# Two transformer blocks on one core: small TensorE products laid out as runs on parts of the array

## The chip, the cores and the metric

One Trainium2 chip, one core of it. A core has TensorE for matrix products (PE in the profile, its weight loads PEld), VectorE (DVE), ScalarE (ACT), GpSimd (POOL) and SyncE (SP), which here issues nearly all the loads. The metric is the device time of one execution in microseconds (us). A time is the median of three executions; beside it stands one profiled execution, with its own time and a span from its first to its last instruction.

## The reference, cut to what matters

Everything is float32; 256 tokens of width 1024 (the "latent" stream x) and 256 tokens of context. First come two layers of a first block, then two layers of a second block:

```
for i in 0, 1:                                   # first block
    x = x + concat(diff_attention, moba_attention) @ w_out[i]
    x = x + conv_ffn(rms_norm(x))                # 1024 -> 2 x 2816 -> 1024
ada[i] = silu(c or c_ctx) @ w_ada[i] + b_ada[i]  # second block: 1024 -> 6144, for latent and context
for i in 0, 1:                                   # shift, scale and gate come from ada[i]
    mix of modulate(x): layer 0 a recurrence (rwkv) and a window attention,
                        layer 1 two attentions that also see the context
    x = x + gate * rms_norm(mix @ w_out_2[i])
    x = x + gate * rms_norm(relu(modulate(x) @ w_ff1[i])**2 @ w_ff2[i])
```

Layer 0 of the second block also runs on the context (its attention, its recurrence, its MLP). q and k of all heads are 64 wide; an attention is q times k transposed, a softmax, and the product with v. A layer of the first block has a "diff" attention (4 heads, each with two score maps, whose difference weighs a v of 128) and a "moba" attention (8 heads of 64).

## The kernel before, in words

The program is traced by a tile framework. A planner then orders each engine's instructions: it takes what is ready by priority (the program's order, unless a context raises it) and by modelled durations and free slots, and each engine runs its list in that order. Two contexts steer it: `tc.issue_after(i)` puts what is traced inside, as far as it is on the engine of `i`, behind `i` in that engine's list (it does not wait for `i` to finish, and it does not hold loads or other engines); `tc.high_priority()` raises the priority.

Buffers come from three lanes, each with named kinds of slots and PSUM banks: `lat` for the latent stream, `cx` for the context, `sd` ("side") for the modulation. A "big" slot holds 128 x 1024 floats, a "mid" slot 128 x 512. Weight matrices are split in two parts (`whi`, `wlo`), and activations too, so that one float32 product takes three passes of products (`proj`, `feat_block`, `down`, lines L292 to L310 and L746 to L748). All other products are plain float32; in the trace such a product is two passes, that is two MATMUL and two LDWEIGHTS records.

What the change touches:

- **Modulation** (`ada`, products on L778). For each of 12 blocks of 512 columns of `w_ada[i]`, eight products, one for each 128 rows: the 32 columns of `sT` (two of them used) against 128 x 512 of weights. Product k writes the 32 partitions `32*(k%4)` on of one PSUM bank, so k and k+4 add up in the same strip. Then a copy (`asb`, L780), four transposes (`adaT`, L784) and a reduction. Argument `a` is the rows of 128 in one load: 2 in `context1` (blocks 0 to 3 of layer 0, big slots of `cx`), 1 in `rest` (its blocks 4 to 11) and in `side` (layer 1, blocks 0 to 9), both in mid slots of `sd`, and 2 in the last two blocks.
- **Scores.** `pad_q` makes two copies of the transposed q, `qa` with zeros below and `qb` with zeros above, so that one head of a pair meets a full 128-row `kT` that holds both heads. Each head takes two products into one bank (`S`: L528 and L529 in `causal_softmax`, L901 in `attend`, L970 in `attend_self`).
- **Values.** The two heads of a pair write the two halves (64 partitions) of one bank: `om` (L647, L648), `oB` (L954 in `attend`, L1001 in `attend_self`).
- **Recurrence** (`rwkv_group`): eight steps, in each of which products of G and uv (L1372) and of AR and the state (L1377) go into one bank, and a later product updates the state (L1417).

The order of the program: `first_norm`, set-ups, `context1`, `first_layer(0)`, `conv_ffn(0)`, `rest`, `first_layer(1)`, `side`, `conv_ffn(1)`, `second_block`. The planner moves parts of `rest`, `side` and the context's work among the rest.

Of the kernel before, what the change touches and what calls it, by code (L numbers as in the profile page):

```python
# [24 lines left out]
CTX = {"cf": 1, "big": 8, "mid": 12, "small": 24, "raw": 4, "whi": 3, "wlo": 3, "wide": 8, "gC": 1}  # L25
SIDE = {"big": 2, "mid": 6, "small": 4}
# [162 lines left out]
class Net:  # L189
# [217 lines left out]
    def pad_q(self, L):  # L407
        nc = self.nc
        qa = L.big([128, 4, 256], name="qa")
        qb = L.big([128, 4, 256], name="qb")  # L410
        nc.gpsimd.memset(qa[64:128], 0.0)
        nc.gpsimd.memset(qb[0:64], 0.0)
        return qa, qb

    def q_T(self, L, xn, gain, qa, qb):

        nc = self.nc
        for t in range(2):
            ps = L.pB("qT")
            pv = ps.rearrange("p (k f) -> p k f", k=4)  # L420
            for j in range(4):
                nc.tensor.transpose(pv[:, j], xn[t][:, j * 128:(j + 1) * 128], self.ident)
            o = slice(t * 128, (t + 1) * 128)
            ga, gb = (gain, gain) if isinstance(gain, float) else (gain[0:64], gain[64:128])
            nc.scalar.activation(qa[0:64, :, o], pv[0:64], AF.Copy, scale=ga)
            nc.vector.tensor_scalar(qb[64:128, :, o], pv[64:128], gb, None, op0=OP.mult)
# [97 lines left out]
    def causal_softmax(self, q, kT, j, bias):  # L524

        nc, L = self.nc, self.lat
        s = L.pA("S")
        nc.tensor.matmul(s[:, 0:128], q[:, j, 0:128], kT[:, j, 0:128], start=True, stop=True)  # L528
        nc.tensor.matmul(s[:, 128:384], q[:, j, 128:256], kT[:, j, 0:256], start=True, stop=True)  # L529
# [24 lines left out]
    def first_layer(self, i, x, act=None):  # L554
# [15 lines left out]
        def qkv(n, jq):  # L570

            qa, qb = self.pad_q(L)
            self.q_T(L, self.head_norm(L, project(n)), self.qg8[:, 2 * i + jq:2 * i + jq + 1], qa, qb)
# [8 lines left out]
            yield qa, qb, kT, v  # L582
# [3 lines left out]
        def diff_att(qa, qb, kT, v, o):  # L586
            def soft(h):
                bias = load_bias(h)
                p0, s0 = self.causal_softmax(qa, kT, h, bias)
                p1, s1 = self.causal_softmax(qb, kT, h, bias)  # L590
# [39 lines left out]
        def moba_att(qa, qb, kT, v):  # L630
            def soft(p):
                ls = []
                for e, q in ((0, qa), (1, qb)):
                    l, s = self.causal_softmax(q, kT, p, load_bias(4 + 2 * p + e))
# [7 lines left out]
            def weigh(p, ls):  # L642
                pts = [self.causal_PT(l) for l in ls]
                o = L.pA("om")
                for e, pt in enumerate(pts):
                    h, oe = 2 * p + e, o[e * 64:(e + 1) * 64]
                    nc.tensor.matmul(oe[:, 0:256], v[:, 0, h * 64:(h + 1) * 64], pt[:, 0:256], start=True, stop=False)  # L647
                    nc.tensor.matmul(oe[:, 128:256], v[:, 1, h * 64:(h + 1) * 64], pt[:, 256:384], start=False,  # L648
                                     stop=True)
# [101 lines left out]
    def ada(self, L, i, a, blocks=range(12)):  # L751
# [19 lines left out]
        for nb in blocks:  # L771
            ps = L.pA("ada")
            for kb in range(0, 8, a):
                raw = (L.big if a == 2 else L.mid)([128, a, 512], name="adaw")
                nc.sync.dma_start(raw, self.plain_rows(w)(kb, a, nb * 512, 512))
                for k in range(kb, kb + a):
                    j = k % 4
                    nc.tensor.matmul(ps[32 * j:32 * j + 32], self.sT[:, k], raw[:, k - kb], start=k < 4, stop=k >= 4)  # L778
            sb = L.mid([128, 512], name="asb")
            nc.scalar.activation(sb, ps, AF.Copy)  # L780

            ps = L.pA("adaT")
            for c in range(4):
# [269 lines left out]
    def rest(self):  # L1053
        for _ in self.ada(self.sd, 0, 1, range(4, 12)):
            pass
# [766 lines left out]
```

## Time and profile before

| | |
|---|---|
| median of 3 runs | 2090.18 us (2087.27 to 2091.03) |
| the profiled execution | 2091.09 us, its span 2089.2 us |
| busy in the span | PE 92%, PEld 76%, DVE 65%, ACT 49%, POOL 45% |
| mean granted TensorE clock | 0.962 |
| DMA | 351.08 MB, mean 168 GB/s |

Busy time of PE is the union of its MATMUL records; records of neighbouring matmuls overlap, so what a group costs PE is read from one start to the next start. "x16" counts MATMUL records, two for each float32 product.

### The profile page before, as it was taken

The numbers are of one execution on the slowest core, as the hardware profiler recorded it, in microseconds if no ns is written. First come the engines' busy times: TensorE is split into PE (matmuls) and PEld (weight loads), VectorE is DVE, ScalarE is ACT, GpSimd is POOL, SyncE is SP. The second block draws the span as 40 slices with busy tenths as digits, with TensorE's granted clock in tenths as the row PEclk, the third lists the DMA queues.
The fourth block names the chain that finished last, engine by engine and source line by source line (L and its number), as shares of the span: only waits on it lengthen the run. The fifth ranks groups of instructions, "written<-read, shape, count | busy, mean of one in ns | idle before, by whom it ended". The sixth has DMA issues, their size and how long they took to land.

```text
span 2089.2 us, 37719 instructions
## 1 busy us (share of the span) xinstructions
PE 1913.3 (92%) x14178; PEld 1591.1 (76%) x14178; DVE 1362.9 (65%) x2855; ACT 1025.7 (49%) x1990; POOL 934.0 (45%) x621
## 2 busy tenths in 40 slices
PE   6989999989998889999898887898699989998998
PEld 4567868888665558899787777787599978776997
DVE  5475388856787645786679878557764467656444
ACT  4455455545454435465465553344454454655443
POOL 3235544693232444444535355545364555113453
PEclk9999999999899999999999999999899999999999
DMA  9857555445455665665563334426465536234562
GB/s 339 309 173 229 155 185 168 151 141 160 144 171 185 189 193 167 196 219 155 176 214 90 103 107 137 135 82 202 152 217 181 188 100 219 71 112 149 184 199 74
DMA packets 270815, 351.08 MB, mean 168 GB/s; under 512 B 43150, under 2 KB 195469, under 8 KB 270632
## 3 DMA queue, kind: packets, MB, share of 16 engines
q1 hardware_dynamic: 267992, 343.32, 51.7%
q0 software_dynamic: 1968, 4.33, 0.7%
q8 instruction: 112, 1.84, 0.4%
q10 hardware_dynamic: 672, 1.02, 0.1%
q14 instruction: 71, 0.58, 0.1%
HBM read 334.04 MB, written 14.55 MB: 167 GB/s over the span
## 4 chain that ended last, share of the span: by engine, by line
PE 44%; DVE 12%; issue 3%; ACT 3%; DMA 2%; POOL 1%; SPq 0%; DVEq 0%; ACTq 0%; POOLq 0%
PE f L310 4%; PE acc L748 3%; PE f L308 3%; PE acc L746 3%; PE acc L747 3%; PE f L309 3%; POOL wlo L269 1%; PE S L901 1%; DVE T L1335 1%; PE up L308 1%; PE g L308 1%; PE up L310 1%; PE g L309 1%; PE g L310 1%; PE up L309 1%
## 5 line engine op out<-in xcount | busy, mean ns | idle before, releaser
L269 POOL TENSOR_TENSOR wlo<-raw,whi 128x1024 fp32r<-128x1024 f32 (+2 forms) x408 | 787.1, 1945 | 985.9 <-ACT whi L265 824.5
L265 ACT ACTIVATE whi<-raw 128x1024 fp32r<-128x1024 f32 (+2 forms) x600 | 507.8, 882 | 139.5 <-issue 35.0
L269 DVE TENSOR_TENSOR wlo<-raw,whi 128x1024 fp32r<-128x1024 f32 x192 | 310.7, 1620 | 108.8 <-ACT whi L265 95.0
L308 PE MATMUL f<-ah,whi 128*128 128x256 f32 x768 | 221.7, 289 | 14.1 <-ACT whi L265 13.9
L310 PE MATMUL f<-ah,wlo 128*128 128x256 f32 x768 | 223.4, 291 | 4.6 <-POOL wlo L269 4.6
L309 PE MATMUL f<-al,whi 128*128 128x256 f32 x768 | 221.3, 288 | 0.3 <-DVE al L383 0.2
L746 PE MATMUL acc<-whi,hh 128*128 128x512 f32 x432 | 168.8, 393 | 2.1 <-ACT hh L461 2.1
L747 PE MATMUL acc<-wlo,hh 128*128 128x512 f32 x432 | 169.2, 392 | 0.0
L748 PE MATMUL acc<-whi,hl 128*128 128x512 f32 x432 | 165.3, 390 | 0.4 <-DVE hl L462 0.4
L308 PEld LDWEIGHTS f<-ah,whi 128*128 128x128 f32 x768 | 149.5, 195 | 17.9 <-ACT whi L265 14.7
L310 PEld LDWEIGHTS f<-ah,wlo 128*128 128x128 f32 x768 | 149.3, 194 | 9.1 <-POOL wlo L269 5.8
L309 PEld LDWEIGHTS f<-al,whi 128*128 128x128 f32 x768 | 149.5, 195 | 2.9 <-DVE al L383 0.8
L1583 DVE TENSOR_TENSOR r<-r 128x512 f32<-128x512 f32 x48 | 39.6, 824 | 126.5 <-ACT r L1582 125.1
L1582 ACT ACTIVATE r<-f 128x512 f32<-128x512 f32 x48 | 28.7, 597 | 186.3 <-PE f L310 179.6
L293 PE MATMUL prj<-wlo,ah 128*128 128x512 f32 (+1 forms) x272 | 107.8, 397 | 3.2 <-DVE wlo L269 2.1
L292 PE MATMUL prj<-whi,ah 128*128 128x512 f32 (+1 forms) x272 | 108.5, 404 | 0.4 <-DVE bt L499 0.4
L310 PE MATMUL g<-ah,wlo 128*128 128x256 f32 x352 | 102.1, 290 | 6.2 <-POOL wlo L269 6.2
L294 PE MATMUL prj<-whi,al 128*128 128x512 f32 (+1 forms) x272 | 105.4, 396 | 1.4 <-DVE al L383 1.4
L778 PE MATMUL ada<-adaw,kept 128*32 128x512 f32 x384 | 98.3, 643 | 8.0 <-DMA adaw<-in_w_ada_dram 7.7
L308 PE MATMUL g<-ah,whi 128*128 128x256 f32 x352 | 102.7, 292 | 0.4 <-DVE kept L786 0.4
L310 PE MATMUL up<-ah,wlo 128*128 128x256 f32 x352 | 101.4, 288 | 1.2 <-POOL wlo L269 1.2
L308 PE MATMUL up<-ah,whi 128*128 128x256 f32 x352 | 102.3, 291 | 0.0
(473 smaller groups left out, 4873.8 us busy)
## 6 DMA issues: line engine op xcount, KB each, us to landing
raw<-in_w_ff_dram SPq DMA_DIRECT2D x128, 512.0 KB, 4.3
raw<-in_w_up_dram SPq DMA_DIRECT2D x88, 512.0 KB, 4.7
adaw<-in_w_ada_dram SPq DMA_DIRECT2D x144, 256.0 KB, 5.0
raw<-in_w_ff_dram SPq DMA_DIRECT2D x128, 256.0 KB, 4.2
raw<-in_w_in_dram SPq DMA_DIRECT2D x48, 512.0 KB, 4.9
raw<-in_w_down_dram SPq DMA_DIRECT2D x44, 512.0 KB, 4.3
adaw<-in_w_ada_dram SPq DMA_DIRECT2D x24, 512.0 KB, 7.5
raw<-in_w_out_dram SPq DMA_DIRECT2D x24, 512.0 KB, 4.2
```

The lines of the kernel that those rows point to most:

```text
L265: nc.scalar.activation(hi, raw, AF.Copy)
L269: eng.tensor_tensor(lo, raw, hi.bitcast(F32), op=OP.subtract)
L292: nc.tensor.matmul(ps[t][:, :n], ah, wh[:, k], start=st, stop=False)
L293: nc.tensor.matmul(ps[t][:, :n], ah, wl[:, k], start=False, stop=False)
L294: self.last = nc.tensor.matmul(ps[t][:, :n], al, wh[:, k], start=False, stop=en)
L308: nc.tensor.matmul(pv[:, j], wh[:, k % a, c], ah, start=first, stop=False, skip_group_check=skip)
L309: nc.tensor.matmul(pv[:, j], wh[:, k % a, c], al, start=False, stop=False, skip_group_check=skip)
L310: nc.tensor.matmul(pv[:, j], wl[:, k % a, c], ah, start=False, stop=k == 7, skip_group_check=skip)
L746: nc.tensor.matmul(acc[t][n], hh[:, k, c], wh[:, n], start=st, stop=False)
L747: nc.tensor.matmul(acc[t][n], hh[:, k, c], wl[:, n], start=False, stop=False)
L748: self.last = nc.tensor.matmul(acc[t][n], hl[:, k, c], wh[:, n], start=False, stop=en)
L778: nc.tensor.matmul(ps[32 * j:32 * j + 32], self.sT[:, k], raw[:, k - kb], start=k < 4, stop=k >= 4)
```

## The change

`ada` asks for all four loads of a block (two rows of 128 each, big slots, of which the side lane now has five), then traces its eight products as one run in the order of rows 6, 7, 4, 5, 2, 3, 0, 1; the copy, the transposes and the reduction after them are at high priority. A run (`Net.run`) puts each product behind the one before it, at high priority. `side` puts the PE instructions of layer 1's modulation behind the last product of `conv_ffn(0)`. q is kept once (`qT`), and `pair_scores` multiplies its upper and lower 64 partitions with those of kT, into two banks, as one run that alternates between the heads, head 1 first. The value products of a pair are runs too, alternating, head 1 first. The lanes `cx` and `sd` get the slot `asb`; `attend_self` is changed as `attend` is. In the recurrence the G products of a step are put behind the state update of the step before.

```diff
-SIDE = {"big": 2, "mid": 6, "small": 4}
+SIDE = {"mid": 4, "small": 4, "big": 5, "asb": 1}
...
-    def pad_q(self, L):
-        qa = L.big([128, 4, 256], name="qa")
-        qb = L.big([128, 4, 256], name="qb")
-        nc.gpsimd.memset(qa[64:128], 0.0)
-        nc.gpsimd.memset(qb[0:64], 0.0)
...
+    def q_T(self, L, xn, gain):
+        q = L.big([128, 4, 256], name="qT")
...
-            nc.scalar.activation(qa[0:64, :, o], pv[0:64], AF.Copy, scale=ga)
-            nc.vector.tensor_scalar(qb[64:128, :, o], pv[64:128], gb, None, op0=OP.mult)
+            if t == 0:
+                nc.scalar.activation(q[:, :, o], pv, AF.Copy, scale=gain)
+            else:
+                nc.vector.tensor_scalar(q[:, :, o], pv, gain, None, op0=OP.mult)
...
+    def pair_scores(self, ss, parts):
+        rows = [slice(e * 64, (e + 1) * 64) for e in range(2)]
+        self.run([lambda o=o, q=q, k=k, e=e, r=r: self.nc.tensor.matmul(ss[e][:, o], q[r], k[r], start=True, stop=True)
+                  for o, q, k in parts for e, r in ((1, rows[1]), (0, rows[0]))])
+
+    def causal_scores(self, q, kT, j):
+        L = self.lat
+        ss = [L.pA("S") for _ in range(2)]
+        self.pair_scores(ss, [(slice(o, o + n), q[:, j, c:c + 128], kT[:, j, 0:n])
+                              for c, o, n in ((0, 0, 128), (128, 128, 256))])
+        return ss
...
             def weigh(p, ls):
...
+                self.run([lambda e=e, kt=kt: product(e, kt) for kt in range(2) for e in (1, 0)])
...
-            for kb in range(0, 8, a):
-                raw = (L.big if a == 2 else L.mid)([128, a, 512], name="adaw")
-                nc.sync.dma_start(raw, self.plain_rows(w)(kb, a, nb * 512, 512))
-                for k in range(kb, kb + a):
-                    j = k % 4
-                    nc.tensor.matmul(ps[32 * j:32 * j + 32], self.sT[:, k], raw[:, k - kb], start=k < 4, stop=k >= 4)
-            sb = L.mid([128, 512], name="asb")
+            raws = []
+            for kb in range(0, 8, 2):
+                raws.append(L.big([128, 2, 512], name="adaw"))
+                nc.sync.dma_start(raws[-1], self.plain_rows(w)(kb, 2, nb * 512, 512))
+            order = [6, 7, 4, 5, 2, 3, 0, 1]
+            self.run([lambda k=k, m=m: nc.tensor.matmul(ps[32 * (m % 4):32 * (m % 4) + 32], self.sT[:, k],
+                                                        raws[k // 2][:, k % 2], start=m < 4, stop=m >= 4)
+                      for m, k in enumerate(order)])
+            with self.tc.high_priority():
+                sb = L.tile("asb", [128, 512], F32, "asb")
...
+        def scores(j, t):
+            ss = [pS("S") for _ in range(2)]
+            self.pair_scores(ss, [(slice(b * 256, (b + 1) * 256), q[:, j, t * 128:(t + 1) * 128], kTs[b](j))
+                                  for b in range(2)])
+            return ss
...
-            for kt in range(4):
-                for e in range(2):
-                    nc.tensor.matmul(o[e * 64:(e + 1) * 64, t * 128:(t + 1) * 128], vs[kt // 2](j, e, kt % 2),
-                                     pts[e][:, kt], start=kt == 0, stop=kt == 3)
+            self.run([lambda kt=kt, e=e: nc.tensor.matmul(
+                o[e * 64:(e + 1) * 64, t * 128:(t + 1) * 128], vs[kt // 2](j, e, kt % 2), pts[e][:, kt],
+                start=kt == 0, stop=kt == 3) for kt in range(4) for e in (1, 0)])
...
-    def side(self):
-        for _ in itertools.chain(self.ada(self.sd, 1, 1, range(10)), self.setup_odd(self.sd)):
+    def side(self, after):
+        self.behind(self.ada(self.sd, 1, range(10)), after)
+        for _ in self.setup_odd(self.sd):
             pass
+    def run(self, products):
+        last = products[0]()
+        for p in products[1:]:
+            with self.tc.issue_after(last.ins), self.tc.high_priority():
+                last = p()
+        return last
...
...
+            with self.tc.issue_after(update.ins) if i else nullcontext():
...
         net.conv_ffn(0, x)
+        end = net.last
         net.rest()
...
-        net.side()
+        net.side(end)
```

## Rows read from the trace of the kernel before

**Rows 1.** The page, part 1: busy us, share of the span, instructions.
```profile
PE 1913.3 (92%) x14178; PEld 1591.1 (76%) x14178; DVE 1362.9 (65%) x2855; ACT 1025.7 (49%) x1990; POOL 934.0 (45%) x621
```
**Rows 2.** Busy by stretch: length, PE, PEld, DVE, ACT, POOL, clock, DMA, GB/s.
```profile
26.00:320.00 294.00, 277.93 (x1593) 204.06 (x1592) 175.62 (x466) 152.82 (x343) 126.39 (x93) 0.98 0.66 218
...
540.00:800.00 260.00, 235.60 (x1559) 155.20 (x1559) 174.13 (x497) 116.73 (x257) 86.36 (x91) 0.92 0.57 180
...
1080.00:1475.00 395.00, 349.68 (x3536) 307.64 (x3535) 288.90 (x582) 184.36 (x417) 198.27 (x134) 0.94 0.43 129
...
1740.00:1875.00 135.00, 131.19 (x814) 103.77 (x813) 82.87 (x247) 80.07 (x186) 31.61 (x16) 1.00 0.44 138
```
**Rows 3.** Busy time by stretch of the modulation's products alone (L778).
```profile
26.00:320.00 294.00, 44.69 (x192) 0.98 0.66 218
...
540.00:800.00 260.00, 49.75 (x160) 0.92 0.57 180
...
1875.00:2089.20 214.20, 3.85 (x32) 0.96 0.47 151
```
**Rows 4.** Busy time by stretch of the products of L901 alone.
```profile
1080.00:1475.00 395.00, 19.41 (x64) 0.94 0.43 129
...
1740.00:1875.00 135.00, 32.80 (x128) 1.00 0.44 138
```
**Rows 5.** PE's timeline from 127.5 us: start us, us, instruction, records.
```profile
127.79 1.05 PE L778 MATMUL ada<-adaw,kept 128*32 128x512 f32 x2
128.77 0.49 PE L528 MATMUL S<-kT,qa 128*128 128x128 f32 x2
...
130.28 1.06 PE L778 MATMUL ada<-adaw,kept 128*32 128x512 f32 x8
131.27 0.38 PE L292 MATMUL prk<-whi,ah 128*128 128x256 f32 x1
```
**Rows 6.** PE's timeline from 72.9 us.
```profile
73.02 1.92 PE L778 MATMUL ada<-adaw,kept 128*32 128x512 f32 x16 [0.35 <-DVE bt L499]
```
**Rows 7.** PE's timeline from 1818 us.
```profile
1818.16 0.43 PE L954 MATMUL oB<-pt,vb 128*64 128x128 f32 x2
1818.52 0.66 PE L933 MATMUL PT<-kept,L 128*128 128x128 f32 x4
...
1819.45 0.59 PE L901 MATMUL S<-kept,qb 128*128 128x256 f32 x2
1819.88 0.59 PE L901 MATMUL S<-kTc,qb 128*128 128x256 f32 x2
...
1820.84 0.54 PE L954 MATMUL oB<-pt,vb 128*64 128x128 f32 x5
...
1821.85 0.70 PE L901 MATMUL S<-kTb,qa 128*128 128x256 f32 x2
...
1829.49 0.54 PE L954 MATMUL oB<-pt,vb 128*64 128x128 f32 x5
...
1830.52 0.66 PE L933 MATMUL PT<-kept,L 128*128 128x128 f32 x4
```
**Rows 8.** PE's timeline from 812 us: products on quarters of the array.
```profile
813.01 0.46 PE L1377 MATMUL P<-kept,AR 64*64 64x64 f32 x16
```
**Rows 9.** The chain from 750 to 800 us, shares by line.
```profile
by line: PE ada L778 26.7%; PE g L308 9.6%; PE g L309 9.2%; PE g L310 8.0%; PE nT L370 5.2%; PE up L309 5.2%; PE up L308 5.2%; PE up L310 4.5%; PE P L1393 3.4%; PE adaT L784 3.1%; PE P L1406 2.5%; ACT sqj L340 2.5%; PE P L1372 2.4%; DVE rst
```
**Rows 10.** The chain from 1262 to 1300 us, shares by line.
```profile
by line: DVE T L1335 41.8%; DVE Ttmp L1333 34.4%; issue 11.2%; DVE cf L1561 6.3%; DVE xs L1387 2.2%; DVE kept L1381 1.9%; DVE r L1583 1.6%; DVE fl L462 1.6%
```
**Rows 11.** Waits, PE and PEld: in total us, times, longest us.
```profile
PEld ada L778 <- DMA adaw<-in_w_ada_dram: 13.9, 15, 2.9
```
**Rows 12.** Loads of the modulation: count, KB each, median us to landing.
```profile
adaw<-in_w_ada_dram SPq DMA_DIRECT2D x144, 256.0 KB, 5.0
...
adaw<-in_w_ada_dram SPq DMA_DIRECT2D x24, 512.0 KB, 7.5
```
**Rows 13.** Busy time by stretch: the start.
```profile
26.00:105.00 79.00, 75.06 (x367) 46.27 (x365) 44.11 (x109) 32.86 (x59) 24.44 (x17) 1.00 0.93 323
```

More of the change, by code (lines that the diff above doesn't have):

```diff
@@ L2 @@
 import math
-from contextlib import ExitStack
+from contextlib import ExitStack, nullcontext
 import numpy as np
@@ L644, in weigh, with product @@
                 o = L.pA("om")
[L645 to L649, printed above, removed]
+                def product(e, kt):
+                    h, q = 2 * p + e, slice(128 * kt, 256)
+                    return nc.tensor.matmul(o[e * 64:(e + 1) * 64, q], v[:, kt, h * 64:(h + 1) * 64],
+                                            pts[e][:, 256 * kt:256 + 128 * kt], start=kt == 0, stop=kt == 1)
+                self.run([lambda e=e, kt=kt: product(e, kt) for kt in range(2) for e in (1, 0)])
                 self.split_to(his[1][:, p], los[1][:, p], o[:, :256])
@@ L748, in down, with ada @@
                 self.last = nc.tensor.matmul(acc[t][n], hl[:, k, c], wh[:, n], start=False, stop=en)
-    def ada(self, L, i, a, blocks=range(12)):
+    def ada(self, L, i, blocks=range(12)):
         self.mark(f"ada{i}")
@@ L938, in attend @@
         groups = [(j, t) for j in range(4) for t in range(2)]
-        now = []
+        now, ss = [], scores(0, 0)
         for e in range(2):
-            now.append(soft(0, 0, e))
+            now.append(soft(ss[e], 0, 0, e))
             yield
@@ L945, in attend @@
             after, pts = [], []
+            ss = scores(*groups[i + 1]) if i < 7 else None
             for e in range(2):
-                if i < 7:
-                    after.append(soft(*groups[i + 1], e))
+                if ss:
+                    after.append(soft(ss[e], *groups[i + 1], e))
                 pts.append(turn(now[e]))
@@ L998, in out @@
             o = L.pA("oB")
-            for kt in range(2):
-                for e in range(2):
-                    nc.tensor.matmul(o[e * 64:(e + 1) * 64, :256], v[:, kt, e * 64:(e + 1) * 64], pts[e][:, kt],
-                                     start=kt == 0, stop=kt == 1)
+            self.run([lambda kt=kt, e=e: nc.tensor.matmul(
+                o[e * 64:(e + 1) * 64, :256], v[:, kt, e * 64:(e + 1) * 64], pts[e][:, kt], start=kt == 0, stop=kt == 1)
+                for kt in range(2) for e in (1, 0)])
             put(chunk0 + j, o[:, :256])
@@ L1053, in rest, with behind @@
     def rest(self):
-        for _ in self.ada(self.sd, 0, 1, range(4, 12)):
+        for _ in self.ada(self.sd, 0, range(4, 12)):
             pass
-    def side(self):
-        for _ in itertools.chain(self.ada(self.sd, 1, 1, range(10)), self.setup_odd(self.sd)):
-            pass
-    def behind(self, steps):
-        with self.tc.issue_after(self.last.ins):
+    def side(self, after):
+        self.behind(self.ada(self.sd, 1, range(10)), after)
+        for _ in self.setup_odd(self.sd):
+            pass
+    def run(self, products):
[4 more added lines that the diff above has]
+        return last
+    def behind(self, steps, after=None):
+        with self.tc.issue_after((after or self.last).ins):
             for _ in steps:
@@ L1614, in context1 @@
         L = self.cx
-        for _ in self.ada(L, 0, 2, range(4)):
+        for _ in self.ada(L, 0, range(4)):
             pass
@@ L1720, in heads @@
         def heads():
-            qa, qb = self.pad_q(L)
             ps = project(0, 512)
             yield
-            self.q_T(L, rows(ps), 0.125, qa, qb)
+            q = self.q_T(L, rows(ps), 0.125)
             yield
@@ L1757, in second_block @@
         self.lat_out(1, act, x)
-        self.behind(self.ada(self.cx, 1, 2, range(10, 12)))
+        self.behind(self.ada(self.cx, 1, range(10, 12)))
         self.lat_mlp(1, x)
```

82 lines of the change are left out of this document (34 added, 48 removed).

## The prediction

> **What bounds the kernel now.** I read the page first. PE is busy for 92% of the span, the next engine, DVE, for 65% [rows 1]. That is an average, so the second view is the busy time by stretch, in the four stretches where the changed products run [rows 2]. The reader should compare PE with the next engine in each. In 26 to 320 us (first layer's attention, with the context's start) PE is busy for 277.9 of 294 us, in 540 to 800 us (second layer's attention) for 235.6 of 260, in 1740 to 1875 us (the last attention) for 131.2 of 135, and no other engine passes 70% in any of them. In 1080 to 1475 us, the recurrence beside the window attention and the context's MLP, PE has 349.7 of 395 us and DVE 288.9, so two engines are close.
>
> The third view, busy time by stretch of one line, says how much of that is work that the change touches: the modulation's products take 44.7 us of the first stretch, 49.8 of the second, and 3.9 at the end, 98.3 in all [rows 3]; the scores of L901 take 19.4 and 32.8 us [rows 4].
>
> The fourth view is PE's timeline, and it carries the argument. A single product of the modulation (two records) takes 1.05 us; four of them (eight records), which write four different strips of the bank, take 1.06 us [rows 5]; eight in a row (one block) take 1.92 us [rows 6]. Strips run side by side, and the array is paid for once. Where the planner has put one product between other work, it pays for the whole array and uses a quarter.
>
> Last, the chain of waits: from 750 to 800 us the modulation's products are 26.7% of it [rows 9], so there they do set the time. From 1262 to 1300 us the chain is DVE's triangular solve (L1333 and L1335, 76%) [rows 10], so there PE's work does not.
>
> **The change part by part.** *Modulation.* Work is not removed, it is packed. A block costs 1.92 us as a run [rows 6]. The first stretch holds 192 records, 12 blocks at 16: 12 x 1.92 = 23.0 instead of 44.7, saves 21.7 us. 540 to 800 us holds 160, 10 blocks: 19.2 instead of 49.8, saves 30.6. The last two blocks (32 records in 3.85 us) are runs already and save nothing [rows 3]. Sum 52.3 us.
>
> *Scores.* A product of 256 columns costs 0.43 us from start to start [rows 7] and one of 128 columns half of that, 0.22 (estimate, same rate). The padded q makes half of each product zeros. After the change two heads use 64 rows each. No row shows two halves of 64 rows with 128 columns. The bounds are: no overlap, saving nothing, and full overlap, half. The nearest row has products on 64 x 64 quarters, 16 records of 64 columns in 0.46 us [rows 8]; at the rate of 0.43 us for two records of 256 columns they would take 16 x 0.054 = 0.86 one after another. So parts with different rows do overlap, and I take full overlap, less a start for each run. That start is read from single products: 1.05 us against 0.86 us for the further four strips of a block (1.92 less 1.06) [rows 5, 6], of which some 0.07 overlaps what follows (the next start is 0.98 after), so 0.12 us a run. L901 has 64 products in 16 groups in the last attention: 64 x 0.43 / 2 = 13.8, less 16 x 0.12, is 11.9. The window attention has 32 in 8 groups: 5.9. In a layer of the first block 8 groups (four heads, four pairs) have two products of each size, 1.30 us (one group with its start is seen to take 1.51, from 128.77 to 130.28 [rows 5]); after, 0.65 + 0.12: saves 0.53 x 8 = 4.2 a layer. The context's four groups: 4 x (0.86 - 0.12) = 3.0. Sum 29.2 us.
>
> The Trainium skill, TensorEngine Tiling (Array Packing), section Tiling Modes, speaks against this part: a change of the tiling mode drains the array. Each of the 44 score runs stands between full products, so by that rule it pays on the way in and out; the 0.12 us a run taken here would be that drain, and without it the sum would be 5.3 us larger. The skill's page TensorE: Matmul & The Clock Gate, Part 3, gives 3.07 times for four row tiles where four were ideal. By that figure a pair would gain 1.54 times and not 2, and the scores would save some 10 us less; no row here shows the pair.
>
> *Values.* In the last attention a group's eight products come as one (0.36 us to the next start) and seven (1.01 us); where all eight come together they take 1.03 us [rows 7]. Saves 0.34 a group: 16 groups, 5.4 us; in the window attention 8 groups, 2.7. The moba pairs issue one head after the other, 1.30 us by the prices above; alternating 0.65 + 0.12: 0.53 x 4 = 2.1 a layer. The context's values I leave out. Sum 12.3 us.
>
> *Loads and slots.* In the side lane the 144 loads of 256 KB become 72 of 512 KB; landing takes 7.5 us for the size used now by the context, 5.0 for the small one [rows 12]. Five big slots hold one block and a quarter, so three loads of the next block wait until a run has freed its four slots; behind them in SP's queue stand the loads of weights, whose slots hold four blocks ahead. PE's wait is what changes most: a run begins with the rows loaded last, so PE, which takes its list in order, meets at most one wait a block, but with all its later products behind it. Before, PE's weight loads waited 13.9 us for these loads, 2.9 at most [rows 11]. I cost it at nothing more: 22 waits of under 1 us would be 10 us or so, and the same planner places the run. If that cover fails, the rival below has the price.
>
> *At nothing:* the zeroing of q leaves POOL, which is idle 55% of the time [rows 1]; q's copies become one for each half of the tokens instead of two; modulation of layer 1 behind the end of `conv_ffn(0)`, since its products stand after 540 us in any case [rows 3]; the high priority of the copy and transposes; and the G products behind the state update. If the last were wrong it would add one such batch (0.6 to 1.1 us, estimate from the 0.46 of rows 8 upward) to each of 7 steps, some 8 us of a chain that other PE work surrounds.
>
> PE work saved by stretch: 26 to 320 us: 21.7 + 4.2 + 2.1 + 3.0 = 31.0. 540 to 800: 30.6 + 4.2 + 2.1 = 36.9. 1080 to 1475: 5.9 + 2.7 = 8.6. 1740 to 1875: 11.9 + 5.4 = 17.3. In all 93.8 us.
>
> What of it reaches the end? Bounds are nothing and all. In the last attention PE is busy 97% and the next engine 61% [rows 2], and I take 0.85: 14.7. In 26 to 320 PE is at 95%, but the loads use 93% of the DMA engines until 105 us [rows 13], and single products of the modulation also filled gaps that will now stand empty; in 540 to 800 PE is at 91% and DVE at 67%, with softmax chains that come forward next. I take two thirds in both: 20.7 and 24.6. In 1080 to 1475 the solve on DVE is late next; a third, 2.9. Sum 62.9 us. The profiled execution took 2091.1 us, so 2028.2; the median is 0.9 below it, so **2027 us**. Its own range is 2005 to 2050.
>
> **The rivals.**
> - *All of it counts.* For it: PE is at 91% or more in three of the stretches [rows 2], and the modulation stands on the chain [rows 9]. Against: the solve [rows 10]. 2090.2 - 93.8 = 1996 us.
> - *Halves by rows do not overlap.* Then the scores give nothing and pay their starts: converted as above, (4.2 + 3.0) x 0.67 + 4.2 x 0.67 + 5.9 / 3 + 11.9 x 0.85 = 19.7, and 44 x 0.12 x 0.75 = 4 more: 2027 + 24 = 2051. Against it: rows 8. A smaller form, the 1.54 times of the skill, lies inside the forecast's range: 10 x 0.67, some 7 us later.
> - *Another bound comes forward* in the two first-block stretches: loads in the first, softmax chains in the second. A quarter instead of two thirds of 67.9 us costs 28: 2055; with nothing there, and only the last attention's 14.7, 2075.
> - *Slower: PE stands at the head of runs.* Loads come later than planned and everything behind a run in PE's list waits. It decides from 62.9 / 22 = 2.9 us of stall a block. At 5.0 us, a landing time [rows 12], 22 blocks cost 110 and leave 47: 2137. For it: DMA is at 93% early on [rows 13], and some waits reached 2.9 us [rows 11]. Against: the mean of those 15 waits is 0.9 us.
>
> **How the numbers follow.** A measurement of this kernel tells a change of about 0.2% (4 us) from none. Chances: forecast 0.55, all of it 0.16, no overlap 0.08, another bound 0.13 (of which 0.04 so strong that no change is seen), slower 0.08. So faster 0.88, same 0.04, slower 0.08. The range leaves out the slower case, the worst of another bound and the far end of all of it: 1988 to 2070.
>
> **What would show it.** The modulation's records in 24 groups of 16, near 46 us of PE in all; L901's successor at half its busy time, 26 us and some; PE's busy total down by about 90 us, its idle time up by about 30. If PE's total falls and the span does not, the conversion was wrong, and the waits before `PT`, `nT` and the first record of each modulation run say where it went. If the paired scores take as long as now, the overlap was wrong. Long waits of PE for `adaw` would mean the slower rival.

## The result and the profile after

The changed kernel takes 2105.5 us (median of 7 runs, 2098.0 to 2115.1) against 2091.0 beside it (7 runs): 1.0071 times, 95% interval 1.0055 to 1.0087. It is slower by some 15 us, where the prediction had it faster by 63. The profiled execution took 2106.56 us, its span is 2104.7.

The page after, part 1 and two rows of part 2 (the span in 40 slices, in tenths):

```profile
PE 1893.6 (90%) x14178; PEld 1598.9 (76%) x14178; DVE 1384.1 (66%) x2847; ACT 1031.9 (49%) x1982; POOL 899.3 (43%) x605
...
PE   6789978999898699999999999798699999998998
...
PEclk9889989999998757999999999899899999989999
```

PE's busy time fell by 20 us only [rows 1], and the clock row dips to 5 near 750 us. Busy time by stretch, the stretches of [rows 2]:

```profile
26.00:320.00 294.00, 256.85 (x1572) 192.42 (x1572) 170.36 (x458) 147.97 (x334) 119.58 (x85) 0.91 0.66 224
540.00:800.00 260.00, 218.96 (x1507) 155.04 (x1507) 171.44 (x466) 108.31 (x248) 94.93 (x104) 0.80 0.53 167
...
1080.00:1475.00 395.00, 356.48 (x3714) 319.45 (x3713) 295.34 (x613) 193.59 (x439) 209.41 (x142) 0.94 0.47 141
1740.00:1875.00 135.00, 125.27 (x820) 96.29 (x819) 93.16 (x270) 79.78 (x190) 32.31 (x19) 0.95 0.38 123
```

The granted clock (third column from the end) fell from 0.98 to 0.91 and from 0.92 to 0.80 in the first two, and from 1.00 to 0.95 in the last. Busy time at half clock hides what was saved, so I split each trace's span in three. **Work** is the time from each PE record's start to the next one's (at most to its own end) times the clock granted then, that is, at full clock; **clock** is what half clock adds; **idle** is the rest between PE's first record and its last (some 19 us of each span stand before and behind them). (Busy time by clock of a windows row gives nearly the work: 214.02 x 0.80 = 171 for the second attention below.)

| span and its parts, us | span | work | clock | idle |
|---|---|---|---|---|
| before | 2089.2 | 1859.3 | 53.6 | 156.8 |
| after | 2104.7 | 1773.5 | 119.6 | 192.4 |

The work fell by 85.8 us, near the 93.8 that the prediction had, though not by its terms alone (see below). Clock took 66.0 of it back and idle 35.6; 101.6 in all, 16 more than was saved. By phase, each ending with the last product of an output projection or of a network: the first attention grew from 265.7 to 278.0, the first network from 267.6 to 287.5, the second attention from 210.9 to 248.6; the second network shrank from 256.4 to 221.3 (the layer-1 modulation has moved), the recurrence's phase from 479.2 to 468.4, its MLP from 210.9 to 203.4, the last attention from 190.0 to 187.9. So 35 us are lost by 1035 us and 19 won after it.

PE's timeline after, at some places (L785 is what L778 was, L523 the score runs, L652 the value runs):

```profile
63.36 1.92 PE L785 MATMUL ada<-adaw,kept 128*32 128x512 f32 x16
...
75.88 3.64 PE L785 MATMUL ada<-adaw,kept 128*32 128x512 f32 x16 [7.39 <-DMA adaw<-in_w_ada_dram]
...
171.70 0.93 PE L523 MATMUL S<-kT,qT 64*128 64x128 f32 x8
...
175.52 0.48 PE L523 MATMUL S<-kT,qT 64*128 64x128 f32 x2
...
176.59 0.92 PE L523 MATMUL S<-kT,qT 64*128 64x128 f32 x6
...
219.89 0.87 PE L652 MATMUL om<-pt,v 128*64 128x256 f32 x8
...
723.54 3.64 PE L785 MATMUL ada<-adaw,kept 128*32 128x512 f32 x16 [3.95 <-DMA adaw<-in_w_ada_dram]
...
733.27 3.35 PE L785 MATMUL ada<-adaw,kept 128*32 128x512 f32 x16 [4.24 <-DMA adaw<-in_w_ada_dram]
...
754.50 1.55 PE L652 MATMUL om<-pt,v 128*64 128x256 f32 x8
...
786.43 0.80 PE L292 MATMUL wo<-whi,yh 128*128 128x512 f32 x1
...
790.01 0.63 PE L294 MATMUL wo<-whi,yl 128*128 128x512 f32 x1
...
791.08 0.40 PE L294 MATMUL wo<-whi,yl 128*128 128x512 f32 x1
```

A block as a run takes 1.92 us as in [rows 6], and 3.64 where PE waited for its loads and the clock had fallen. A score run in one piece takes 0.93; where something stands between its first product and the rest it takes 0.48 and 0.92. From 746.6 to 790 us, behind a wait of 1.6 us, PE idles for 0.1 us and yet runs at half clock: a value run (`om`) takes 1.55 us there, 0.87 at full clock. The stretch as a row:

```profile
746.60:790.00 43.40, 43.31 (x376) 30.26 (x377) 20.22 (x81) 17.13 (x59) 7.48 (x12) 0.50 0.19 51
```

PE's waits after, and then PE's wait for the modulation's loads before:

```profile
PE nT L370 <- DVE xn L362: 42.2, 12, 8.7
PE ada L785 <- DMA adaw<-in_w_ada_dram: 15.6, 3, 7.4
PE kT L429 <- DVE hn L401: 12.1, 2, 6.7
PE qT L415 <- DVE hn L401: 11.5, 3, 5.8
```

```profile
PE ada L778 <- DMA adaw<-in_w_ada_dram: 7.7, 5, 2.6
```

With the weight loads, which waited 13.9 us before [rows 11] and 0.3 after, the waits for these loads are shorter in sum than they were (15.9 against 21.6 us), but PE's stand in three pieces of up to 7.4 us.

### The profile page after: what moved, and what is told of

Same layout as the page of the kernel before. It is cut to its first block, busy times and chain, and to the rows that moved or that the text cites. A ratio compares the mean times of both kernels' runs of the same rounds, so it can differ in the third digit from the quotient of the medians.

```text
span 2104.7 us, 37530 instructions
## 1 busy us (share of the span) xinstructions
PE 1893.6 (90%) x14178; PEld 1598.9 (76%) x14178; DVE 1384.1 (66%) x2847; ACT 1031.9 (49%) x1982; POOL 899.3 (43%) x605
## 5 line engine op out<-in xcount | busy, mean ns | idle before, releaser
L269 POOL TENSOR_TENSOR wlo<-raw,whi 128x1024 fp32r<-128x1024 f32 (+2 forms) x408 | 768.1, 1894 | 1008.3 <-ACT whi L265 947.7
L265 ACT ACTIVATE whi<-raw 128x1024 fp32r<-128x1024 f32 (+2 forms) x600 | 520.1, 886 | 349.4 <-PE f L309 98.0
L269 DVE TENSOR_TENSOR wlo<-raw,whi 128x1024 fp32r<-128x1024 f32 x192 | 264.2, 1377 | 237.1 <-ACT whi L265 227.8
L308 PE MATMUL f<-ah,whi 128*128 128x256 f32 x768 | 222.5, 291 | 10.6 <-ACT whi L265 10.1
L1603 DVE TENSOR_TENSOR r<-r 128x512 f32<-128x512 f32 x48 | 94.7, 1974 | 28.2 <-ACT r L1602 26.1
L309 PE MATMUL g<-al,whi 128*128 128x256 f32 x352 | 103.5, 294 | 3.1 <-DVE al L378 3.1
L752 PEld LDWEIGHTS acc<-whi,hh 128*128 128x128 f32 x432 | 82.0, 190 | 25.4 <-ACT hh L456 9.6
```

The costliest lines, as they stand in the source:

```text
L265: nc.scalar.activation(hi, raw, AF.Copy)
L269: eng.tensor_tensor(lo, raw, hi.bitcast(F32), op=OP.subtract)
L308: nc.tensor.matmul(pv[:, j], wh[:, k % a, c], ah, start=first, stop=False, skip_group_check=skip)
L309: nc.tensor.matmul(pv[:, j], wh[:, k % a, c], al, start=False, stop=False, skip_group_check=skip)
L752: nc.tensor.matmul(acc[t][n], hh[:, k, c], wh[:, n], start=st, stop=False)
L1603: nc.vector.tensor_tensor(r, r, r, op=OP.mult)
```

## The experiments

Ratios are to the kernel before, run beside each. The edits are shown abridged. The theories: **A**, PE's work got too thin where other chains set the length; **B**, the parts of the array themselves lower the clock; **C**, the new order of PE's list costs the time.

**Layout by itself** (e1). A kernel that leaves the network out and runs each kind of product back to back between full ones:

```diff
+        for f, n in ((single, 32), (strips, 32), (pairs, 64), (padded, 64), (values, 128), (turns, 128)):
+            f(n); warm(24)
+        for _ in range(12): pairs(2); turns(8); values(4)      # the last attention's mix
+        for _ in range(12): padded(4); turns(8); values(4)
```

> This kernel leaves the whole network out: it copies x and runs, on PE alone and without waits, stretches of some 20 us of one kind of float32 product each, with full 128x128x512 products between them. Theory A (PE became sparser, the layout is harmless): every kind holds a granted clock of 1.00 in its stretch; a pair of 64-row halves with 256 columns costs 0.43 us, four strips 0.86 to 0.9 us. Theory B (products on parts of the array do not hold the clock even when nothing waits): the stretches of strips, pairs or values fall to 0.50, those of padded products stay at 1.00.

The granted clock is 1.00 through the whole span. Four strips take 0.86 us (27.6 for 32 rounds), as long as one; a pair of halves 0.435 us, as a padded product alone (0.43). In the mix, from start to start:

```profile
353.25 1.09 PE L72 MATMUL val<-w,x 128*64 128x128 f32 x16
354.28 1.13 PE L62 MATMUL pair<-w,x 64*128 64x256 f32 x8
355.34 1.09 PE L78 MATMUL turn<-ident,w 128*128 128x128 f32 x8
356.37 1.09 PE L72 MATMUL val<-w,x 128*64 128x128 f32 x16
```

Two pairs between other products take 1.06 us where alone they take 0.87, so a run pays 0.19 us for its start, not 0.12. The group takes 3.12 us, with padded scores 3.82. B falls, and so does the rival that halves by rows do not overlap. The Trainium skill, TensorE: Matmul & The Clock Gate, Part 3, measured 3.07 times where four were ideal; these two halves reach 2.0 of 2. The Trainium skill, TensorEngine Tiling (Array Packing), Tiling Modes, has a change of mode drain the array; the 0.19 us agrees with that.

**One part at a time** (e2, e3) and **no saving by packing** (e4): the kernel before with the modulation's part; the changed kernel with the modulation as before; the changed kernel with every modulation product 128 columns wide, which then cannot stand beside another:

```diff
-        self.sT = self.keep([128, 8, 32], F32, name="sT")
+        self.sT = self.keep([128, 8, 128], F32, name="sT")
...
-            matmul(ps[32 * (m % 4):32 * (m % 4) + 32], self.sT[:, k], raws[k // 2][:, k % 2], start=m < 4, stop=m >= 4)
+            matmul(ps, self.sT[:, k], raws[k // 2][:, k % 2], start=m == 0, stop=m == 7)
```

> The kernel before with the modulation's part of the change alone (runs, loads, slots, gate). Theory A: PE's work at full clock falls by about 41 us, half of the added half-clock time of the change (150 us in all) appears here, mostly before 130 us and between 560 and 760 us, and the time is within 12 us of before. Theory B: the same fall of the clock, but inside and right behind the runs also where PE does not wait. Theory C (the new order alone costs, whatever the packing): slower than before by 10 us or more, with PE's idle time up by over 25 us.

> The changed kernel with the modulation put back as before (single products, small loads): scores, values and the recurrence's order as changed. Theory A: here the single products still fill PE, so the half-clock time stays near the 159 us of before, and the time falls by 20 to 30 us. Theory B: half-clock time grows in the attention stretches all the same (over 200 us), and the time is within 10 us of before. Theory C: slower than before.

> The changed kernel, but each of the modulation's products uses all 128 columns of the array (96 of them zeros) and the eight of a block add up in one strip, so that a run takes eight times 0.86 us and not 1.9. That is 24 x 5 = 120 us more PE work in the same order. Theory A: the work stands where PE was waiting at the lower clock, so the time grows by clearly less than 120 us, about 30 to 60, and the half-clock time falls from 309 us to under 230. Theory C: the order costs what it cost, half-clock time stays near 300 us, and the time grows by 90 us or more.

The modulation alone: 2101.2 us, 1.0050 (1.0029 to 1.0071). The pairs, with the change's line in the recurrence, which e3 keeps: 2093.7, 1.0021 (1.0009 to 1.0033). So each part is slower by itself. The time of e2 and its idle time, 35 us more than before, fit A and C alike; e3 is slower, as C had it. The wide products: 2172.3, 1.0388 (1.0368 to 1.0408): 121.6 us more work than in the changed kernel cost 67 us, above A's range and below C's. Of these, 56 us are lost before the second attention begins. In the second attention they cost nothing; the row of the kernel before, that of the wide kernel, and that of the changed one:

```profile
533.30:744.20 210.90, 189.78 (x1220) 127.55 (x1218) 151.09 (x436) 96.77 (x218) 76.29 (x75) 0.92 0.55 174
```

```profile
621.40:868.40 247.00, 230.31 (x1569) 155.51 (x1568) 157.34 (x450) 103.28 (x240) 84.50 (x94) 0.97 0.53 167
```

```profile
565.50:814.10 248.60, 214.02 (x1471) 149.95 (x1469) 160.40 (x438) 102.73 (x239) 93.25 (x103) 0.80 0.54 170
```

Some 52 us more work there (224.5 against 172.0, 51 of it the modulation's) fit into the same 247 us: in the order of the changed kernel PE's work does not set that phase's length, and with more of it the clock stays up (0.97 against 0.80). In that phase this is A. The Trainium skill, TensorE: Matmul & The Clock Gate, section HAM oscillation, tells of bursts of products between waits that fall to the low clock every time; rows 723.54 and 733.27 above show such runs.

**One line of order** (e5), and **the second block's pairs alone** (e6):

```diff
+            with self.tc.issue_after(update.ins) if i else nullcontext():   # e5: the G products of a step
...
-        qa, qb = self.pad_q(L)                                              # e6: gqa_q, attend, attend_self,
+        return self.q_T(L, xq, scale)                                       # last attention, as in the change
```

> The kernel before with one line of the change: the G products of a recurrence step are put behind the state update of the step before. Theory A (PE became too sparse in the first block): nothing of that is here, so the time stays within 5 us of the kernel before and the first block's phases within 2 us. Theory C (a new order from the planner, whatever its cause, costs the time): the planner's list changes here too, so single phases should move by 5 us or more in either sign, though the work is the same.

> The kernel before with the paired scores, single q and value runs in the second block alone (window attention, last attention, the context's attention); modulation, first block and recurrence as before. Theory A: there the softmax chains do not set the end and PE does, so the gain seen in the second block of the kernel with the pairs alone (11 us to the end of layer 0's mix, 4 us in its MLP, 1 to 3 us after) appears without the loss of the first block: 2070 to 2080 us, PE work 17 to 25 us less at full clock, clock cost within 8 us of the kernel before. Theory C: the first block's phases lengthen by 5 us or more again, though nothing in them but the context's four groups is changed, and the time is 2085 us or more.

The one line is a gain by itself: 2086.0 us, 0.9966 (0.9953 to 0.9979); the recurrence's phase takes 469.0 us instead of 479.2. PE's list is that of before up to the recurrence, and yet the second attention took 213.3 us instead of 210.9; so phases of single executions can differ by 2.4 us under the same list. The second block's pairs lose: 2136.4, 1.0206 (1.0181 to 1.0231), and not in the second block. The first network, of which no product was edited, took 318.8 us instead of 267.6; before, and then e6:

```profile
265.70:533.30 267.60, 253.47 (x1987) 215.22 (x1986) 196.96 (x333) 140.13 (x256) 147.32 (x113) 0.97 0.51 159
```

```profile
274.10:592.90 318.80, 280.37 (x2275) 232.75 (x2274) 217.39 (x432) 145.50 (x273) 137.14 (x108) 0.94 0.44 138
```

The planner moves the context's attention, which was edited, among the first block's work, and dealt all of it anew. That speaks for C, and against reading any one phase as the worth of one edit.

**Shorter runs** (e7), **no gate** (e8), both on the modulation's part alone:

```diff
+            for half in range(2):                    # e7: two loads, a run of four, two loads, a run of four
...
+        for _ in itertools.chain(self.ada(self.sd, 1, range(10)), self.setup_odd(self.sd)):   # e8: side as before
```

> The modulation's part alone, as in the earlier run, but each block as two runs of four products with two loads each. Theory A: the modulation's PE work grows by some 22 x 0.2 = 4 us only and stays packed, so the time stays at 2095 to 2105 us with a clock cost near 75 us. Theory C in the form of the waits at the head of a run: the waits of PE for the modulation's loads fall from 17.9 us to under 8 and PE's idle time from 192 to under 180, and the time is 2085 to 2093 us.

> The modulation's part alone, as in the earlier run, but layer 1's modulation is not put behind the end of the first convolution network. Theory A: its products still come as runs of 1.9 us, so within 5 us of 2101. Theory C in the form of the gate: the planner may spread the runs over the first network too, the second attention's phase (222.9 us with the gate, 210.9 before) comes back to 215 or less and the time to 2093 or less.

Halves: 2105.4 us, 1.0062 (1.0045 to 1.0080). The waits for the loads, in e2 and then in e7:

```profile
PE ada L779 <- DMA adaw<-in_w_ada_dram: 17.9, 3, 8.0
```

```profile
PE ada L778 <- DMA adaw<-in_w_ada_dram: 6.8, 4, 3.1
...
PEld ada L778 <- DMA adaw<-in_w_ada_dram: 5.7, 4, 4.0
```

PE's wait fell by 11 us, and by 6 with that of the weight loads (0.6 in e2), and the time did not fall, so the waits at the heads of runs are not the main loss. Without the gate: 2143.4, 1.0247 (1.0227 to 1.0267), outside A's range and the opposite of what C in that form expected: the first network takes 336.6 us. Beside e2 the gate, which the prediction costed at nothing, is worth some 42 us.

**The saving without the order** (e9, e10, e11). Here the planned lists of the kernel before stay as they are, in every engine; only after planning are operands of some products replaced, so that they take less of PE. Their sums are then no longer those of the network: e9 leaves out most of half of each modulation sum, e10 has rougher scores.

```diff
+    cut = lambda a, n: a.__replace__(ap=[*a.ap[:-1], (a.ap[-1][0], n)], bass_ap=None)
+    high = lambda a: a.__replace__(dtype=bfloat16, ap=[(2 * s, n) for s, n in a.ap], offset=2 * a.offset + 1, bass_ap=None)
...
+            if n:            # modulation, k >= 4: 64 columns of 512
+                b.instructions[i] = copy.replace(p, ins=[cut(p.ins[0], n), *p.ins[1:]], outs=[cut(p.outs[0], n)])
+            elif n == 0:     # second score product of a head: upper halves, one pass
+                b.instructions[i] = copy.replace(p, ins=[high(a) for a in p.ins])
```

> The kernel before with its planned lists as they are (order, loads, waits, slots unchanged); only after planning are the second four products of each modulation block cut from 512 to 64 columns (448 of 512 columns of that half of the sum are left out). So work leaves PE, 25 to 40 us at full clock, about what packing takes away, and nothing moves. Theory A (the first block cannot use thinner PE work: other engines' chains set its length and the clock falls in the gaps): time within 6 us of the kernel before, clock cost and idle time up by nearly what was removed. Theory C (the saving is worth what the prediction said, and the planner's new order loses it): two thirds of the removed work comes off, 15 to 27 us, so 2064 to 2075 us.

> Again the kernel before with its planned lists unchanged; after planning, the second score product of each head (in both blocks and the context) reads only the upper 16 bits of q and k, which makes it one pass of TensorE instead of two slower ones: some 0.3 us less for each of 88 products, 25 to 28 us of PE work, near what pairing was to save (29.2). Its scores are rougher, no work else is left out. Theory A: only the last attention (12 of the 28 us) can use it, so 6 to 12 us off, 2079 to 2085. Theory C: the prediction's shares, 18 to 20 us off, 2070 to 2073.

> Both cuts of the two runs before, in the unchanged lists of the kernel before: 50 to 68 us of PE work less. Theory A: 2075 to 2085 us, the first block within 6 us of the kernel before. Theory C: 33 to 47 us off, 2043 to 2058 us. If the first block gains nothing from either cut but the sum of idle time and clock cost there rises by what was removed, the step of the prediction that turned work into time has failed by itself; if it gains, the new order has taken more than the difference.

| | time | ratio (interval) | work less | gained | clock, idle more |
|---|---|---|---|---|---|
| e9 | 2077.7 | 0.9943 (0.9921 to 0.9965) | 40.9 | 11.9 | 7.1, 13.6 |
| e10 | 2078.2 | 0.9936 (0.9909 to 0.9962) | 26.8 | 13.4 | 1.3, 15.5 |
| e11 | 2063.2 | 0.9885 (0.9859 to 0.9910) | 69.0 | 24.0 | 11.1, 26.2 |

(Gained: one less the ratio, times 2088.07, the median beside them; the rest from the profiled executions, of which those of e9 and e11 are 6.6 and 4.1 us below their medians. By the spans e11 gained 32.0 us, 0.46 of the work.) The cut modulation drops its products to 46.2 us of work, packing to 45.1: the same saving. With the order untouched, 69.0 us of work are worth 24.0 (18.8 to 29.4), 0.35 of it. Neither theory had this: A said too little, C too much. The last attention is the clearest place. Its phase before, with the cut scores, and after:

```profile
1690.70:1880.60 189.90, 178.18 (x1045) 142.30 (x1044) 125.85 (x339) 107.73 (x245) 63.28 (x39) 0.98 0.37 116
```

```profile
1681.70:1869.70 188.00, 171.08 (x1013) 134.90 (x1012) 127.42 (x339) 107.47 (x245) 63.41 (x39) 0.96 0.36 117
```

```profile
1707.20:1895.10 187.90, 173.41 (x1045) 134.79 (x1044) 125.29 (x335) 107.87 (x243) 58.24 (x36) 0.95 0.36 118
```

10.3 us less work gained 2.0 us with the cut, 11.7 us less gained 2.1 with the pairs, in one execution each; both gains are below the 2.4 us by which phases differ under the same list. PE now waits longer for the softmax, with the cut ahead of the scores and with the pairs ahead of the values. In this phase, before, with the cut, and after:

```profile
PE S L901 <- ACT L L921: 1.7, 3, 1.0
...
PE oB L954 <- ACT pt L935: 1.1, 2, 0.8
```

```profile
PE S L903 <- ACT L L925: 5.3, 3, 2.8
```

```profile
PE oB L964 <- ACT pt L946: 4.8, 3, 2.2
```

**A candidate** (e12): single q, paired scores and value runs in the two latent attentions of the second block alone, with e5's line; PE's list as before until the end of the first block.

```diff
-        qa, qb = self.pad_q(L)
+        qs = self.pad_q(L) if L is self.cx else None        # gqa_q: the context keeps both copies
```

> A candidate: the kernel before with the paired scores, single q and value runs in the latent stream's window attention and last attention alone, and the recurrence's G products behind the state update. The planner's list of TensorE is unchanged to row 4897 of 9646 (the end of the first block). Theory A: the last attention gives 3 to 8 us beside the recurrence order's 7: 2074 to 2082 us. Theory C: phases up to 1000 us are the same within 2 us, since their lists are, and the second block's phases gain what the kernel with the pairs alone gained there (14 us): 2073 to 2080. Either way the first block's 35 us are not lost here.

2088.0 us, 0.9999 (0.9984 to 1.0015). The first block is the same (999.5 us against 1000.6), as both theories said, but the candidate fails: what e5's line had gained is gone. In the last attention 10.6 us less work came with 10.6 more of clock and 3.9 more idle, and the phase takes 193.8 us, 3.8 more than before.

**Does the clock come back?** (e13, which leaves the network out.) A wait of some 15 us, one kind back to back, full products, for ten kinds:

```diff
+        for f, n in ((tiny, 96), (quarters, 150), (turns, 150), (wide_values, 48), (pairs, 72), (strips, 36),
+                     (single, 36), (mix, 9), (lambda n: mix(n, strips), 7), (full_, 36)):
+            gap(); f(n); warm(30)
```

> Leaves the network out. TensorE waits some 14 us for a chain on VectorE, then runs one kind of product back to back for 15 to 40 us, then full 128x512 products; ten such stretches, one for each kind (32x32 tiles, 64x64 tiles, transposes, value products, score pairs, strips in fours, single strips, the mix of the second attention's end, that mix with strips, full products), and before them the mix straight behind full products. Theory A (only the gaps cost clock): in each stretch the granted clock is back at full within some 7 us of the first product, whatever the kind. Theory B2 (small products do not bring a fallen clock back, as the second attention's end at half clock from 746 to 790 us lets one think): in the stretches of small tiles, transposes and the mix the clock stays at half until the full products come, while strips, or the mix with strips, bring it back.

Windows of this kernel (no ACT column): the wait before the 32x32 tiles, their first part and the rest, then the same two parts of the transposes and of single strips:

```profile
134.60:149.40 14.80, 1.74 (x2) 0.18 (x2) 12.43 (x18) 0.00 (x0) 0.50 0.00 0
149.40:151.60 2.20, 2.20 (x81) 2.09 (x84) 0.00 (x0) 0.00 (x0) 0.50 0.03 7
151.60:168.60 17.00, 10.84 (x701) 9.94 (x693) 0.00 (x0) 0.00 (x0) 1.00 0.01 4
...
273.00:274.50 1.50, 1.50 (x7) 1.33 (x7) 0.00 (x0) 0.00 (x0) 0.50 0.00 0
274.50:290.00 15.50, 15.50 (x144) 15.50 (x143) 0.00 (x0) 0.00 (x0) 1.00 0.00 1
...
549.00:551.00 2.00, 2.00 (x4) 0.53 (x3) 0.00 (x0) 0.00 (x0) 0.50 0.00 0
551.00:581.00 30.00, 30.00 (x71) 7.50 (x69) 0.00 (x0) 0.00 (x0) 1.00 0.00 1
```

Every kind brings the clock back, and so does the mix. So the kinds of product by themselves do not explain why the changed kernel stays at half from 746.6 to 790 us with PE hardly idle. What its trace shows: up to 786.4 us PE has nothing but small products there (32x32 and 64x64 tiles, transposes, score and value runs); at 786.43 the 128x512 products of the output projection begin, and by 791.08 they take 0.40 us instead of 0.63. The next stretch at half (818.1 to 842.0 us, 1.9 us idle) is alike: small products, and full ones from 839.05 us on. But in e8 such a stretch, 773.3 to 790.3 us, ended among small products. e13's mix has these kinds in longer pieces, 64 records of 32x32 tiles at once where the network has 8 or 16; the finer mixture was not run by itself. The cause stays open.

**Runs with the loads as before** (e14, and e15 with e5's line): two runs of four for each block, loads, slots and the copy's priority as before, no gate.

```diff
-                for k in range(kb, kb + a):
-                    j = k % 4
-                    nc.tensor.matmul(ps[32 * j:32 * j + 32], self.sT[:, k], raw[:, k - kb], start=k < 4, stop=k >= 4)
+                raws += [(k, raw[:, k - kb]) for k in range(kb, kb + a)]
+                if len(raws) == 4:
+                    self.run([lambda k=k, r=r: nc.tensor.matmul(ps[32 * (k % 4):32 * (k % 4) + 32], self.sT[:, k], r,
+                                                                start=k < 4, stop=k >= 4) for k, r in reversed(raws)])
```

> The kernel before with one edit in the modulation: its products are traced as two runs of four (four strips side by side) for each block; loads of 256 KB, slots, no gate and priorities of the copy as before. By the cut lists, 40 us less work is worth about 12 us. Theory C1 (whole-block loads in big slots, the gate and the priorities make the bad order): 2074 to 2084 us. Theory C2 (any new deal of the list loses the single products that filled gaps): 2090 to 2105 us.

> The same with the recurrence's G products behind the state update, which alone gave 0.34%: a candidate. Theory C1: 2068 to 2079 us. Theory C2: 2085 to 2100 us.

2098.1 us, 1.0034 (1.0019 to 1.0050), and with the line 2093.3, 1.0017 (0.9999 to 1.0034). C2: neither the big loads nor the gate nor the copy's priority are needed to lose; runs of four, each product behind the one before it at high priority, are enough. The loss stands in the second attention; its row with the cut lists (e9), then with e14's runs:

```profile
529.70:735.00 205.30, 181.30 (x1219) 129.38 (x1218) 151.31 (x436) 96.41 (x218) 76.69 (x75) 0.90 0.54 178
```

```profile
528.10:757.20 229.10, 190.12 (x1211) 132.04 (x1211) 152.13 (x434) 97.29 (x221) 79.00 (x85) 0.87 0.49 159
```

The same work within 2 us (164.6 and 166.4) takes 24 us longer, 15 of them idle. (Over the whole span e14 has 8.5 us more work than e9.) PE's waits for the modulation's loads are part of that. In this phase, e9 and then e14:

```profile
PE ada L779 <- DMA adaw<-in_w_ada_dram: 4.9, 5, 2.1
```

```profile
PE ada L778 <- DMA adaw<-in_w_ada_dram: 14.2, 4, 6.1
```

## Why the prediction was wrong, point by point

**The packing: right in kind, a fifth too large in size.** The modulation's products went from 86.5 us of work to 45.1, 41.4 less (the 52.3 predicted counted busy time, with half clock and the overlap with neighbours in it); 22 blocks stand as whole runs. Scores fell by 17.3 instead of 29.2: a whole run of 256 columns takes 1.06 us to the next start, 0.98 by the prediction's terms, but 15 of the 44 are cut in two, since the second bank is not free or other work stands between, and those take 0.63 and 1.06. Values gave 15.4, 12.3 predicted. That is 74.1 of the 93.8. The other 11.7 of the 85.8 lie in products that nobody edited (`prj` went from 192.1 to 189.0, with e9's cuts in the order of before it stayed at 192.0), so that the total came near is in part luck. Halves overlap fully (e1), as the quarters do [rows 8].

**The first step that failed: "I take two thirds in both", and 0.85 in the last attention.** With the order held fixed, 0.35 of the work came off (e11; 0.27 to 0.43 by its interval), and 0.2 in the last attention (e10, one execution), where PE was busy for 97% [rows 2]. That share says how much of the time PE works, not how close the next chain stands. There the softmax stood right behind it. At 0.35 the 85.8 us saved would have been worth some 30 us, 2061 us by estimate; that accounts for 33 of the 63 us predicted.

**The second step that failed: "the same planner places the run", costed at nothing.** From those 2061 to 2105.5 is 44 us by estimate, the cost of the new order and what comes with it. Its parts: by the ratios, the modulation alone is 10.4 us slower than before where the cut of equal size was 11.9 faster, 22 us; the pairs alone are 4.4 slower with 27.0 us less work, where the cut scores, with 26.8 less, were 13.4 faster, 18 us. Together 40 of the 44. (e3 has the recurrence's line in it, which by itself gains 7.1; so the pairs' own order costs more than the 18, some 25 us if the two add up.) e14 shows such a cost for the modulation with loads and slots as before and no gate: some 19 us against e9 by the ratios, with 8.5 us more work. In the traces it is idle time and clock: the changed kernel has 9 us more idle than e11 and 55 more of clock, for 17 less of work.

**Clock: left out of the sum.** The prediction took the granted clock as it was. Half clock is 66.0 us of the 101.6 given back. Part of it follows waits that are no longer filled (rows 75.88 and 723.54 above), which so cost twice, as idle and as half clock; but 21.7 us of the 119.6 stand in the stretch from 746 to 790, behind a wait of only 1.6 us.

**The rivals.** "Another bound comes forward" named the right mechanism and priced it too low, 2075 at worst, because it had no term for order or clock. "PE stands at the head of runs" was the one that ended slower, at 2137; its waits are there, 15.6 us in three and 0.7 a block where 5.0 was priced, and e7 cut them without a gain, so it is a part and not the cause. The gate's worth (e8) was not seen at all, and the recurrence's line, put at nothing with 8 us to lose, gained 7.1 (e5).

**Open:** what keeps the clock at half from 746.6 to 790 us, and why each way of grouping makes a worse order. Each part was run in one order or a few, and the planner's deals differ by tens of us in phases whose products nobody edited (e6). That grouping as such is worse than single products, and not only in the orders tried, was not shown.

## What to carry to other kernels

Ask of a saving on the busiest engine how much of it the next chain lets through, and measure it with the order held fixed: cut the operands after planning and leave the lists alone. Products that look wasteful can be good filler; packing them left waits here that cost idle time and clock. Where a planner orders the work, an edit is two changes, its own and the new deal, and here the second was the larger by estimate; the version to keep is the one-line change of order alone (e5), 2086.0 us, 0.34% faster than before.

## What the hardware showed that I had not expected

After a wait of some 15 us every kind of product, 32x32 tiles and transposes among them, brought the clock back to 2.4 GHz early in its stretch (e13). Yet the changed kernel ran 43 us at 1.2 GHz with 0.1 us idle: in these traces the granted clock does not follow from idle time alone. Durations agree with the clock shown (`om` 1.55 us there, 0.87 at full clock).
